# Sums of weights and of normed inputs on GpSimd, two more FFN pairs and one more head group in seven block products, in a two-layer trunk

## The chip, the core and the metric

The kernel runs on one core of a Trainium2 chip. The core has TensorE (PE, matmuls into PSUM), VectorE (DVE), ScalarE (ACT), GpSimd (POOL) and SyncE (SP, which only issues DMAs); each takes its own instructions in order and waits at semaphores for the others. The metric is the device time of one execution in microseconds, as the median of several runs.

## What is computed

A trunk of two layers over one sequence of 512 tokens with 1024 channels, in fp32. Layer 0 mixes tokens by attention, layer 1 by causal pooling; each is followed by a SwiGLU FFN with 2816 hidden channels, and everything stands behind RMSNorms:

```python
for i in range(DEPTH):                    # 2
    j = i // N_MIXERS
    if i % N_MIXERS == 0:
        x = x + dilated_attention_mixer(rmsnorm(x, attn_norm[j]), w_qkv[j], w_attn_out[j])
    else:
        x = x + pooling_mixer(rmsnorm(x, pool_norm[j]), w_pool_in[j], w_pool_group[j], pool_scale[j])
    x = x + swiglu_ffn(rmsnorm(x, ffn_norm[i]), w_ffn_gate_up[i], w_ffn_down[i])
return rmsnorm(x, final_norm)

def swiglu_ffn(h, w_gate_up, w_down):
    gu = h @ w_gate_up
    gate, up = gu[..., :D_FF], gu[..., D_FF:]
    return (jax.nn.silu(gate) * up) @ w_down
```

The attention has 8 heads of 128 channels in each of three groups (windows 128, 512, 2048 with dilations 1, 4, 16). In each head the outputs of the three groups are merged with weights from their softmax denominators.

## The kernel before

**Matmuls.** Every fp32 operand is split in two parts, hi and lo, of a reduced format: `split` copies hi on ACT (L77) and subtracts for lo on DVE (L78). Each product is three matmuls: hi x hi, hi x lo, lo x hi. A plain product (`Product.add`, L254, L255, L257) runs over 8 chunks of 128 channels with 512 tokens at a time.

**Seven block products.** Most products are made in pairs (gate and up of an FFN tile, q and k of a head and group) as a 2 x 2 block product with seven multiplications in place of eight (`seven`, matmuls at L371 to L373 with 256 tokens; `values12` with L483 to L485 for the values). It needs sums of the weight blocks and sums of the normed inputs. A weight pair (`Pair`) is loaded as tiles b, a and c by SP, a DMA issued on POOL (L137) accumulates a further block into b, and then four steps split them: `blocks` (a), `sums` (b), `more`, which first makes two sums in a (L150, L151) and splits it again (called the m split below), and `last` (c). The tiles lie in rings: five split weights (`w`), two halves, four raw tiles of 1024 columns (`raw`), two raw halves. A step runs when the ring has room, a load when the raw rings have. The sums of the inputs are made by `normed`: L434 scales two chunks of inputs into a raw tile h, and L438 to L440 make the sums in a raw tile t. The two functions `prepare`, one in the attention and one in `ffn`, call it for each of 4 pairs of chunks and split the results (h, t, tx in the attention; tb, tt, tn in the FFN).

**Plain ones.** The first pairs of each FFN (`NPLAIN`) and the first groups of head 1 (`NSOLO`) are plain, in the time in which the inputs for the seven block products are prepared. In the FFN one preparation is written after each plain pair.

**Attention.** The work of a head is laid into the products of the next one. `seven` and `values12` call functions at places counted by block products (`after`, filled by `between` and by the dictionary of head 7's values): `scores0` and `scores12` make scores and softmax parts, `merge` the weights of the groups (L614 on DVE puts the statistics in place, L618 on PE swaps partitions, L621 to L631 are small steps, L633 scales the scores of group 0 on DVE and L636 those of the others on ACT), `turn0` and `turn12` transpose (L645), `turn_values` transposes the values (L540), and `output` multiplies. L614 is issued behind the last instruction of the preceding evacuation (`mark`).

What stands where on an engine comes from a scheduler that takes the instructions as they become ready by their priority, so the written order is not the order on the engines.

Of the kernel before, what the change touches and what calls it, by code (L numbers as in the profile page):

```python
# [16 lines left out]
S = 512  # L17
# [15 lines left out]
NF = 4  # L33
H2 = S // 2
K2 = KC // 2
NPLAIN = 6
WARM = 6
NSOLO = 3
DOWN = (6, 5)
BUFS = {"w": 5, "half": 2, "raw": 4, "rawhalf": 2}  # L40
COLS = {"w": D, "half": D // 2, "raw": D, "rawhalf": D // 2}
# [7 lines left out]
def trunk(ctx: ExitStack, tc: tile.TileContext, xT, norms, w_first, w_qk, w_qkp, w_v0, w_v0p, w_v12, w_out, w_pair, w_down, w_pin, w_pgrp,  # L49
          consts, ident_in, invcnt_in, outT):  # L50
    nc = tc.nc
# [24 lines left out]
    def split(hi, lo, v):  # L76
        nc.scalar.activation(hi, v, AF.Copy)  # L77
        nc.vector.tensor_tensor(lo, v, hi.bitcast(F32), op=OP.subtract)  # L78
# [42 lines left out]
    class Pair:  # L121
# [25 lines left out]

        def more(self):
            a, b = self.a.t, self.b.t
            nc.vector.tensor_add(a[:, :S], a[:, :S], b[:, :S])  # L150
            nc.vector.tensor_add(a[:, S:], a[:, S:], a[:, :S])  # L151
            self.b.done()
            self.w["m"] = Held("w")
            split(*self.w["m"].t, a)
            self.a.done()
# [33 lines left out]
    for h in range(HEADS):  # L189
        if h == 0:  # L190
            plain(*[w_qk[u] for u in range(len(QK) - NF)])
        for g in range(3):
            if h == 1 and g < NSOLO:
                plain(*[w_qk[len(QK) - NF + 2 * g + c] for c in range(2)])
            elif h:
                pairs(w_qkp[3 * h - 3 - NSOLO + g])
        if h == 0:
# [7 lines left out]
    def ffn_plan(layer):  # L205
        for hf in range(2):
            for j in range(hf * HALF, (hf + 1) * HALF):
                if j < NPLAIN:
                    plain_gu(layer, j)
# [219 lines left out]
    def normed(layer, k, row):  # L429

        h, t = Held("raw"), Held("raw")
        for i in range(2):
            c = k + i * K2
            nc.vector.scalar_tensor_tensor(h.t[:, i * S:(i + 1) * S], X[c], nrm[:, layer, c:c + 1], row,  # L434
                                           op0=OP.mult, op1=OP.mult)
        hq = h.t.rearrange("p (a b c) -> p a b c", a=2, b=2)
        tq = t.t.rearrange("p (a b c) -> p a b c", a=2, b=2)
        nc.vector.tensor_sub(tq[:, :, 0], hq[:, :, 1], hq[:, 0])  # L438
        nc.vector.tensor_sub(t.t[:, H2:S], t.t[:, :H2], h.t[:, 3 * H2:])
        nc.vector.tensor_add(t.t[:, 3 * H2:], t.t[:, H2:S], h.t[:, S:3 * H2])  # L440
        return h, t

    def halves_of(hi, lo):
# [7 lines left out]
    with tc.tile_pool(name="opool", bufs=1) as opool:  # L451
        early = opool.tile([P, HEADS, S], F32R, tag="o", name="early")
        with tc.tile_pool(name="apool", bufs=1) as apool:
# [307 lines left out]
            def later(f, *a):  # L761
                return lambda: f(*a)

            def between(h, g):

                if g == 0:
                    return {1: [later(merge, h - 1)], 3: [later(turn_values, h - 1)] if h > 1 else []} if h % 2 else {
                        1: [later(output, h - 2)], 2: [later(merge, h - 1)]}
                if g == 1:
                    return {0: [later(turn0, h - 1)], 2: [later(turn12, h - 1)], 4: [later(scores0, h)]}  # L770
                return {2: [] if h % 2 else [later(output, h - 1)]}
# [19 lines left out]
            for h in range(1, HEADS):  # L791
                for g in range(3):
                    if h == 1 and g < NSOLO:
                        for c in range(2):
                            evac(h, 2 * g + c, product(0))
                        for fs in between(h, g).values():
                            for f in fs:
                                f()
                    else:
                        for c in range(2):  # L800
                            QKV[h, g, c] = apool.tile([P, S], F32, name=f"qk{g}{c}")
                        seven(T, QKV[h, g, 0], QKV[h, g, 1], scratch, between(h, g), g == 0)
                if h == 1:
                    whole = opool.tile([P, HEADS, S], F32, tag="o", name="o")
                    o.extend(whole[:, h, :] for h in range(HEADS))
                if h == HEADS - 1:
                    for key in [key for key in held if key[0] == "t"]:
                        give(key)
                    X[:] = [x_tile(k) for k in range(KC)]
                    for k in range(KC):  # L810
                        nc.gpsimd.dma_start(X[k], xT[:, k, :])
                if h % 2 == 0:
                    VT[:] = [apool.tile([P, S], F32, tag=tag, name="vt") for tag in ("row", "o0")]
                    seven(T, *VT, scratch, {0: [later(scores12, h)]}, True)
                elif h < HEADS - 1:
                    QKV[h // 2, 12, 2] = values12({0: [later(scores12, h)]})
                else:
                    QKV[h // 2, 12, 2] = values12({0: [later(scores12, h)], 1: [later(halve, 0), later(halve, 1)],
                                                   2: [later(merge, h), later(halve, 2), later(halve, 3)],
                                                   4: [later(halve, 4), later(halve, 5)]})  # L820
            for k in range(KC):
                give(("h", k))
# [29 lines left out]
    with tc.tile_pool(name="fpool", bufs=2) as fpool:  # L852
# [30 lines left out]
        def ffn(layer, nxt, lead, row):  # L883

            op = nxt - 1

            def gu():
                return lead.pop(0).p if lead else product(op)

            def hidden(j):  # L890
                return act[j]

            def plain_pair(last):
                pg = gu()
                gt = ftile("gt")
                nc.vector.tensor_mul(gt, pg, row)
                pu = gu()
                if last:
                    for k in range(KC):
                        give((op, k))  # L900
                up = ftile("up")
                nc.vector.tensor_mul(up, pu, row)
                activation(gt, up)

            T = {}

            def prepare(k):


                h, t = normed(op, k, row)  # L910
                hq, b22 = h.t.rearrange("p (a b c) -> p a b c", a=2, b=2), h.t[:, 3 * H2:]
                held["t", k, 0], b = slot("tb")
                split(b[:, 0].rearrange("p (a c) -> p a c", a=2), b[:, 1].rearrange("p (a c) -> p a c", a=2), hq[:, :, 0])
                T["11", k], T["21", k] = (tuple(b[:, e, i * H2:(i + 1) * H2] for e in range(2)) for i in range(2))
                for i, names in enumerate((("1", "2"), ("3", "4"))):
                    held["t", k, 1 + i], b = slot("tt")
                    split(b[:, 0], b[:, 1], t.t[:, i * S:(i + 1) * S])
                    for a, name in enumerate(names):
                        T[name, k] = tuple(b[:, e, a * H2:(a + 1) * H2] for e in range(2))
                if k % 2 == 0:  # L920
                    held["t", k, 3], T["n"] = slot("tn")
                n = tuple(T["n"][:, e, k % 2 * H2:(k % 2 + 1) * H2] for e in range(2))
                split(*n, b22)
                T["22", k] = n
                h.done()
                t.done()

            def strassen_pair():
                gt, up = ftile("gt"), ftile("up")
                seven(T, gt, up, ftile)  # L930
                activation(gt, up)

            for hf in range(2):
                act.clear()
                for j in range(hf * HALF, (hf + 1) * HALF):
                    if j < NPLAIN:
                        plain_pair(j == NPLAIN - 1)
                        if 0 < j <= K2:
                            prepare(j - 1)
                    else:  # L940
                        strassen_pair()
                early = [Product(HALF, hidden).add(range(HALF - 1)) for i in range(2)]
                if hf:
                    for key in [key for key in held if key[0] == "t"]:
                        give(key)
                for m in range(KC - 2 if nxt == 4 and hf else KC):
                    if early:
                        f = early.pop(0).add([HALF - 1])
                    else:
                        f = Product(HALF, hidden).add(range(HALF))  # L950
                    if hf and layer == 0:
                        unfold(m, f.p)
                    else:
                        nc.vector.tensor_add(X[m], X[m], f.p)
                    if hf:
                        note(nxt, m)
                if not (hf and nxt == 4):
                    for j in range(HALF):
                        give(("a", j))
            return hidden  # L960
# [118 lines left out]
        t = total(0, add(0, 0, end(0, 0, range(HALF))))  # L1079
# [4 lines left out]
        t = total(1, add(0, 1, f))  # L1084
# [80 lines left out]
```

## Time and profile before

| | |
|---|---|
| median of 3 runs | 1272.15 us (1271.86 to 1273.1) |
| profiled execution | 1271.68 us, span 1269.9 us |
| granted TensorE clock | 0.997 |
| PE busy | 1252.9 us, 99% |
| DVE busy | 922.3 us, 73% |
| ACT busy | 567.6 us, 45% |
| POOL busy | 127.2 us, 10% |
| HBM | 135 GB/s over the span |

The profile is one execution. A row of a timeline has the start in us, the duration in us, the engine, line and operation, output and inputs by name, and in brackets the idle time before it and what ended that. A row with x2 or more takes several equal instructions together. Rows of groups have duration in ns or busy time and the mean; the text ahead of them says which. PE's matmuls are pipelined, so that the distance from start to start is the pitch, and the duration in the row is longer.

### The profile page before, as it was taken

Reading aid. Unit: us, or ns where it says so; the run is one execution under the profiler, and the core shown is the slowest. Engines: PE = TensorE matmul, PEld = TensorE weight load, DVE = VectorE, ACT = ScalarE, POOL = GpSimd, SP = SyncE. Lnnn points to the kernel's source line nnn. Section 1 sums busy time; section 2 is a strip of 40 time slices with the busy share of each in tenths; the row PEclk is TensorE's granted clock in tenths of the full one; section 3 lists DMA queues with packets and bytes.
Section 4 is the critical chain, followed back from the end, with each engine's and each line's share of the span. In section 5 each row is a group of like instructions: output and inputs, shape, how many; then the busy total and the mean of one; then the engine's idle time right before and its main releaser. Section 6 shows DMA issues by size and latency. Waiting matters only on the chain.

```text
span 1269.9 us, 20876 instructions
## 1 busy us (share of the span) xinstructions
PE 1252.9 (99%) x8306; PEld 1154.4 (91%) x8306; DVE 922.3 (73%) x1383; ACT 567.6 (45%) x879; POOL 127.2 (10%) x121
## 2 busy tenths in 40 slices
PE   9999999999999999999999999999999999999997
PEld 7879999999999988889989999888788988999986
DVE  6977788878778846688636887558978853788643
ACT  6444554445445544444424554343444532455331
POOL 1011111102111000001001110000300000110000
PEclk9999999999999999999999999999999999999998
DMA  8335556655755444147446774333124645666322
GB/s 294 100 86 164 133 144 150 165 133 151 182 134 149 118 150 132 52 100 187 129 142 157 183 185 129 99 133 126 41 77 113 172 129 139 171 181 172 92 69 67
DMA packets 67330, 172.45 MB, mean 136 GB/s; under 512 B 6928, under 2 KB 9120, under 8 KB 67232
## 3 DMA queue, kind: packets, MB, share of 16 engines
q1 hardware_dynamic: 48816, 135.97, 33.4%
q0 software_dynamic: 17264, 34.09, 15.8%
q8 instruction: 65, 1.06, 0.3%
q10 hardware_dynamic: 1152, 1.05, 0.2%
q14 instruction: 33, 0.27, 0.1%
HBM read 168.99 MB, written 2.10 MB: 135 GB/s over the span
## 4 chain that ended last, share of the span: by engine, by line
PE 79%; issue 11%; DVE 7%; ACT 2%; POOL 1%; DMA 0%; DVEq 0%; POOLq 0%; ACTq 0%
PE ps L371 12%; PE ps L372 12%; PE ps L373 12%; PE ps L255 10%; PE ps L254 10%; PE ps L257 10%; PE ps L483 2%; PE ps L485 2%; PE ps L484 2%; DVE wlo L78 1%; PE ps L678 1%; PE ps L590 1%; ACT whi L77 1%; POOL rcol L323 1%; DVE n L302 1%
## 5 line engine op out<-in xcount | busy, mean ns | idle before, releaser
L77 ACT ACTIVATE whi<-raw 128x1024 fp32r<-128x1024 f32 (+2 forms) x297 | 295.9, 1001 | 427.7 <-PE ps L255 194.6
L78 DVE TENSOR_TENSOR wlo<-raw,whi 128x1024 fp32r<-128x1024 f32 (+2 forms) x297 | 340.5, 1150 | 153.5 <-ACT whi L77 152.1
L254 PE MATMUL ps<-a,whi 128*128 128x512 f32 (+1 forms) x374 | 141.0, 377 | 0.0
L255 PE MATMUL ps<-a,whi 128*128 128x512 f32 (+1 forms) x374 | 140.9, 377 | 0.0
L257 PE MATMUL ps<-a,wlo 128*128 128x512 f32 (+1 forms) x374 | 140.8, 377 | 0.0
L371 PE MATMUL ps<-tt,whi 128*128 128x256 f32 x384 | 108.7, 283 | 0.0
L372 PE MATMUL ps<-tt,whi 128*128 128x256 f32 x384 | 108.7, 283 | 0.0
L373 PE MATMUL ps<-tt,wlo 128*128 128x256 f32 x384 | 108.7, 283 | 0.0
L137 POOL DMA_DIRECT2D raw<-w_pair x32 | 38.7, 1209 | 445.3 <-DVE wlo L78 173.6
L257 PEld LDWEIGHTS ps<-a,wlo 128*128 128x128 f32 x374 | 70.4, 188 | 13.0
L254 PEld LDWEIGHTS ps<-a,whi 128*128 128x128 f32 x374 | 70.4, 188 | 12.8
L255 PEld LDWEIGHTS ps<-a,whi 128*128 128x128 f32 x374 | 70.4, 188 | 12.7
L372 PEld LDWEIGHTS ps<-tt,whi 128*128 128x128 f32 x384 | 73.7, 192 | 0.0
L371 PEld LDWEIGHTS ps<-tt,whi 128*128 128x128 f32 x384 | 73.7, 192 | 0.0
L373 PEld LDWEIGHTS ps<-tt,wlo 128*128 128x128 f32 x384 | 73.7, 192 | 0.0
L372 PE MATMUL ps<-tb,whi 128*128 128x256 f32 x256 | 72.5, 283 | 0.0
L371 PE MATMUL ps<-h,whi 128*128 128x256 f32 x252 | 72.5, 288 | 0.0
L373 PE MATMUL ps<-tb,wlo 128*128 128x256 f32 x256 | 72.5, 283 | 0.0
L371 PE MATMUL ps<-tb,whi 128*128 128x256 f32 x256 | 72.4, 283 | 0.0
L373 PE MATMUL ps<-h,wlo 128*128 128x256 f32 x252 | 71.3, 283 | 0.0
L372 PE MATMUL ps<-h,whi 128*128 128x256 f32 x252 | 71.3, 283 | 0.0
L254 PE MATMUL ps<-h,whi 128*128 128x512 f32 x160 | 62.7, 392 | 0.0
(280 smaller groups left out, 3423.4 us busy)
## 6 DMA issues: line engine op xcount, KB each, us to landing
raw<-w_pair SPq DMA_DIRECT2D x76, 512.0 KB, 4.3
raw<-w_qkp SPq DMA_DIRECT2D x36, 512.0 KB, 4.2
raw<-w_pair POOLq DMA_DIRECT2D x32, 512.0 KB, 7.2
raw<-w_down SPq DMA_DIRECT2D x32, 384.0 KB, 3.1
raw<-w_down SPq DMA_DIRECT2D x32, 320.0 KB, 2.8
raw<-w_v SPq DMA_DIRECT2D x18, 512.0 KB, 4.2
raw<-w_qkp POOLq DMA_DIRECT2D x18, 512.0 KB, 7.0
rawhalf<-w_pair SPq DMA_DIRECT2D x32, 256.0 KB, 3.4
```

The source lines that it names most:

```text
L77: nc.scalar.activation(hi, v, AF.Copy)
L78: nc.vector.tensor_tensor(lo, v, hi.bitcast(F32), op=OP.subtract)
L137: nc.gpsimd.dma_start(self.b.t.rearrange("p (a c) -> p a c", a=2), self.src[:, None, 3 * S:].to_broadcast([P, 2, S]), accum_op=OP.add)
L254: nc.tensor.matmul(self.p[:, cols], w[0][:, s], mh[:, cols], start=self.done == 0, stop=False)
L255: nc.tensor.matmul(self.p[:, cols], w[0][:, s], ml[:, cols], start=False, stop=False)
L257: nc.tensor.matmul(self.p[:, cols], w[1][:, s], mh[:, cols], start=False, stop=self.done == self.n)
L371: nc.tensor.matmul(dst, w.t[0][:, c], th, start=k == 0, stop=False)
L372: nc.tensor.matmul(dst, w.t[0][:, c], tl, start=False, stop=False)
L373: nc.tensor.matmul(dst, w.t[1][:, c], th, start=False, stop=k == K2 - 1)
L483: nc.tensor.matmul(o, mh, wh, start=k == 0, stop=False)
L484: nc.tensor.matmul(o, mh, wl, start=False, stop=False)
L485: nc.tensor.matmul(o, ml, wh, start=False, stop=k == K2 - 1)
```

## The change

Three things are moved to GpSimd or shifted. The sums L150, L151 and L438 to L440 run on GpSimd in place of VectorE. One more pair of each FFN and one more group of head 1 are made by seven block products. And in the attention the merge after an odd head's start and the turn of the values are placed one block product later, in head 7 the merge is too, and in the FFN each preparation is written one plain pair earlier.

```diff
-NPLAIN = 6
+NPLAIN = 5
-NSOLO = 3
+NSOLO = 2
...
         def more(self):
             a, b = self.a.t, self.b.t
-            nc.vector.tensor_add(a[:, :S], a[:, :S], b[:, :S])
-            nc.vector.tensor_add(a[:, S:], a[:, S:], a[:, :S])
+            nc.gpsimd.tensor_add(a[:, :S], a[:, :S], b[:, :S])
+            nc.gpsimd.tensor_add(a[:, S:], a[:, S:], a[:, :S])
...
-        nc.vector.tensor_sub(tq[:, :, 0], hq[:, :, 1], hq[:, 0])
-        nc.vector.tensor_sub(t.t[:, H2:S], t.t[:, :H2], h.t[:, 3 * H2:])
-        nc.vector.tensor_add(t.t[:, 3 * H2:], t.t[:, H2:S], h.t[:, S:3 * H2])
+        nc.gpsimd.tensor_sub(tq[:, :, 0], hq[:, :, 1], hq[:, 0])
+        nc.gpsimd.tensor_sub(t.t[:, H2:S], t.t[:, :H2], h.t[:, 3 * H2:])
+        nc.gpsimd.tensor_add(t.t[:, 3 * H2:], t.t[:, H2:S], h.t[:, S:3 * H2])
...
-                    return {1: [later(merge, h - 1)], 3: [later(turn_values, h - 1)] if h > 1 else []} if h % 2 else {
+                    return {2: [later(merge, h - 1)], 4: [later(turn_values, h - 1)] if h > 1 else []} if h % 2 else {
...
-                                                   2: [later(merge, h), later(halve, 2), later(halve, 3)],
+                                                   2: [later(halve, 2), later(halve, 3)], 3: [later(merge, h)],
...
                     if j < NPLAIN:
                         plain_pair(j == NPLAIN - 1)
-                        if 0 < j <= K2:
-                            prepare(j - 1)
+                        if j < K2:
+                            prepare(j)
```

The order of the instructions on the engines shows what it moves. First TensorE in head 3, in the first group's products, before:

```order
918 L373 MATMUL ps<-h,wlo 128x256
919 L371 MATMUL ps<-h,whi 128x256
920 L372 MATMUL ps<-h,whi 128x256
921 L373 MATMUL ps<-h,wlo 128x256
922 L371 MATMUL ps<-t,whi 128x256
923 L372 MATMUL ps<-t,whi 128x256
924 L373 MATMUL ps<-t,wlo 128x256
925 L618 MATMUL ps<-far,const 128x32 x2
926 L371 MATMUL ps<-t,whi 128x256
```

And the same place now (t and tx are the sums of the inputs, far the statistics from L614):

```order
959 L373 MATMUL ps<-h,wlo 128x256
960 L371 MATMUL ps<-t,whi 128x256
961 L372 MATMUL ps<-t,whi 128x256
962 L373 MATMUL ps<-t,wlo 128x256
...
969 L371 MATMUL ps<-tx,whi 128x256
970 L372 MATMUL ps<-tx,whi 128x256
971 L373 MATMUL ps<-tx,wlo 128x256
972 L618 MATMUL ps<-far,const 128x32 x2
973 L371 MATMUL ps<-t,whi 128x256
```

The swap stood behind three matmuls with t, and stands behind twelve. On VectorE the instruction that it waits for, L614, had a sum of weights ahead of it:

```order
188 L425 TENSOR_TENSOR vt<-ps,sums 128x4x32x4
189 L426 TENSOR_TENSOR vt<-sums,ps 128x2x32x4
190 L150 TENSOR_TENSOR raw<-raw 128x512
191 L614 TENSOR_TENSOR far<-st,place 128x64
192 L151 TENSOR_TENSOR raw<-raw 128x512
```

Now a lo split stands there:

```order
161 L425 TENSOR_TENSOR vt<-ps,sums 128x4x32x4
162 L426 TENSOR_TENSOR vt<-sums,ps 128x2x32x4
163 L78 TENSOR_TENSOR halflo<-rawhalf,halfhi 128x512
164 L614 TENSOR_TENSOR far<-st,place 128x64
165 L78 TENSOR_TENSOR wlo<-raw,whi 128x1024
```

The sums left VectorE there, and L614 keeps one instruction of that size ahead of it. On GpSimd, from the first RMSNorm (L323) to head 2, there stood before:

```order
10 L323 TENSOR_TENSOR rcol<-var,nhalf 128x4
11 L554 TENSOR_SCALAR b_812<-const 128x256
12 L555 TENSOR_SCALAR b_812<-const 128x128
13 L137 DMA raw<-w_v 128x2x512
14 L558 TENSOR_SCALAR b_815<-const 128x128 x2
15 L137 DMA raw<-w_v 128x2x512
```

There now, of the same stretch, the part from the accumulating DMA of the first pair (the first pair is that of head 1's third group, so its weights are w_qkp):

```order
20 L137 DMA raw<-w_v 128x2x512
21 L150 TENSOR_TENSOR raw<-raw 128x512
22 L151 TENSOR_TENSOR raw<-raw 128x512
23 L438 TENSOR_TENSOR raw<-raw 128x2x256
24 L558 TENSOR_SCALAR b_824<-const 128x128
25 L439 TENSOR_TENSOR raw<-raw 128x256
26 L558 TENSOR_SCALAR b_824<-const 128x128
27 L440 TENSOR_TENSOR raw<-raw 128x256
28 L438 TENSOR_TENSOR raw<-raw 128x2x256
29 L439 TENSOR_TENSOR raw<-raw 128x256
30 L440 TENSOR_TENSOR raw<-raw 128x256
```

The sums of the first pair and of the third and fourth preparations follow each other in one queue, with the slopes of the next head's scores (L558) between them.

## The prediction

> **What bounds the kernel now.** I read the page first, then the waits of TensorE, then a stretch of seven-block products by engine, then TensorE's rows around its waits. The busy time of each engine:
>
> ```profile
> PE 1252.9 (99%) x8306; PEld 1154.4 (91%) x8306; DVE 922.3 (73%) x1383; ACT 567.6 (45%) x879; POOL 127.2 (10%) x121
> ```
>
> TensorE (PE) is the bound: 1252.9 of 1269.9 us. A change can win in two ways only: less matmul time, or fewer of the few waits PE has. The waits of PE, in whole us, times and longest:
>
> ```profile
> PE ps L618 <- DVE far L614: 3.2, 4, 0.9
> PE ps L645 <- ACT s L636: 1.6, 1, 1.6
> PE ps L540 <- DVE nm L575: 0.2, 1, 0.2
> ```
>
> They add up to little, and the largest is the swap of the merge (L618), four times. In the long stretches of seven-block products PE waits for nothing, with VectorE (DVE) at 87%:
>
> ```profile
> core 0: us, PE busy (x) PEld busy (x) DVE busy (x) ACT busy (x) POOL busy (x), PEclk, DMA share, GB/s
> 696.82:747.22 50.40, 50.40 (x422) 50.40 (x421) 43.64 (x62) 26.24 (x35) 6.02 (x5) 1.00 0.72 183
> ```
>
> That stretch is five pairs of the second half of the first FFN, so DVE works 43.64/5 = 8.73 us of each pair's 10.08. Relief of DVE there is worth nothing; only the places where PE waits for DVE count.
>
> **The change part by part.**
>
> *Three more seven-block products in place of plain ones.* The rows give the pitch of each kind:
>
> ```profile
> 520.08 0.39 PE L254 MATMUL ps<-h,whi 128*128 128x512 f32 x1
> 520.76 0.39 PE L254 MATMUL ps<-h,whi 128*128 128x512 f32 x1
> 600.03 0.28 PE L371 MATMUL ps<-tb,whi 128*128 128x256 f32 x1
> 600.39 0.28 PE L371 MATMUL ps<-tb,whi 128*128 128x256 f32 x1
> ```
>
> Three matmuls of 512 columns take 0.68 us, three of 256 columns 0.36. A plain pair has 2 x 8 x 3 = 48 matmuls, 48 x 0.2267 = 10.88 us; a seven-block pair has 7 x 4 x 3 = 84, 84 x 0.12 = 10.08. One pair in each FFN layer and one group of head 1: 3 x 0.80 = **-2.4 us**. Here nothing hides the gain, for PE is the bound.
>
> *The merges one block product later.* The first fence shows PE around the swap of head 3 and what DVE does before it, the second PE at head 7:
>
> ```profile
> 172.87 0.28 PE L373 MATMUL ps<-t,wlo 128*128 128x256 f32 x1
> 173.91 0.60 PE L618 MATMUL ps<-far,const 128*128 128x32 f32 x4 [0.76 <-DVE far L614]
> 172.47 0.65 DVE L426 TENSOR_TENSOR vt<-sums,ps 128x256 f32<-128x256 f32 x1
> 172.95 0.69 DVE L150 TENSOR_TENSOR raw<-raw 128x512 f32<-128x512 f32 x1
> 173.56 0.21 DVE L614 TENSOR_TENSOR far<-st,place 128x64 f32<-128x64 f32 x1
> ```
>
> ```profile
> 435.66 0.28 PE L485 MATMUL ps<-whi,tx 128*128 128x256 f32 x1
> 436.82 0.60 PE L618 MATMUL ps<-far,const 128*128 128x32 f32 x4 [0.88 <-DVE far L614]
> ```
>
> A start gap of 1.04 less the pitch of 0.12 is 0.92 us of standing, at each of the odd heads (three of the four waits); at head 7 it is 1.16 - 0.12 = 1.04. In the order of the changed kernel nine more matmuls stand ahead of the swap at the odd heads, 9 x 0.12 = 1.08 us, and twelve at head 7, 1.44 us. Both are more than the wait, so up to 3 x 0.92 + 1.04 = 3.8 us go. The margin at the odd heads is only 0.16: L150 has left DVE, but a lo split of the same shape now stands in its place ahead of L614, and if GpSimd (POOL) is adding just then, DVE is late by about 0.8 to 1.0 (priced below). POOL will be adding for about a third of the time, so I take off 3 x 0.33 x 0.84 = 0.8: **-3.0 us**, with ends of -1.0 (head 7 alone) and -3.8.
>
> *The sums on POOL instead of DVE.* What they cost on DVE, and the nearest rows of POOL (the page's duration columns; in the first five min/median/max in ns):
>
> ```profile
> L150 DVE TENSOR_TENSOR raw<-raw x61: 678/682/795, 77.9 to 1175.5; 128x512 f32<-128x512 f32 x61
> L438 DVE TENSOR_TENSOR raw<-raw x12: 677/686/693, 40.9 to 975.7; 128x512 f32<-128x512 f32 x12
> L439 DVE TENSOR_TENSOR raw<-raw x12: 409/424/429, 42.1 to 976.9; 128x256 f32<-128x256 f32 x12
> L292 POOL TENSOR_TENSOR acc<-sq 128x512 f32<-128x512 f32 x1 | 1.3, 1330 | 27.3 <-ACT sq L287 27.3
> L1069 POOL TENSOR_TENSOR x<-xg,row 128x256 f32<-128x256 f32 x2 | 1.4, 736 | 1.3 <-ACT row L1065 1.3
> L137 POOL DMA_DIRECT2D raw<-w_pair x32 | 38.7, 1209 | 445.3 <-DVE wlo L78 173.6 <-DMA raw<-w_pair 122.4 <-DVE raw L150 43.3
> ```
>
> L151 is like L150, and L440 like L439. DVE is rid of 2 x 0.682 = 1.37 us per pair and of 0.69 + 2 x 0.42 = 1.53 per prepared pair of chunks. POOL pays 1.33 for 128x512 and 0.74 for 128x256 where it works alone: 2.66 per pair, 2.81 per preparation. The rows where both work at once say more:
>
> ```profile
> 889.41 1.50 DVE L302 SCALAR_TENSOR_TENSOR n<-x,nrm,n 128x512 fp32r<-128x512 f32 x2
> 903.37 2.44 DVE L302 SCALAR_TENSOR_TENSOR n<-x,nrm,n 128x512 fp32r<-128x512 f32 x2
> 905.75 1.75 DVE L1002 TENSOR_TENSOR s<-u 128x512 f32<-128x512 f32 x1
> 896.25 0.66 DVE L1002 TENSOR_TENSOR s<-s 128x512 f32<-128x512 f32 x1
> 903.48 3.47 POOL L292 TENSOR_TENSOR acc<-acc,sq 128x512 f32<-128x512 f32 x2 [11.43 <-ACT sq L287]
> ```
>
> Under two POOL adds that took 3.47 together, DVE's two-input work lost 2.44 - 1.50 = 0.94 and 1.75 - 0.66 = 1.09: about 1.0 us for each POOL add, and POOL's own add grew from 1.33 to 1.74. So per pair in the steady stretch DVE goes from 8.73 to 8.73 - 1.37 + 2 x 1.0 = 9.36 of 10.08, and POOL from 1.21 (its accumulating DMA) to 1.21 + 3.47 = 4.7. Both still fit: **0 us** there. In POOL's queue each accumulating DMA now stands behind an earlier pair's sums, at most 3.5 us later; the rest of the period covers it.
>
> The Trainium skill, GPSIMD Engine Reference, section 4.1, puts two-input elementwise work on VectorE and calls GPSIMD about twice as slow; the rows agree (1.33 against 0.68) and add the stretch to 1.74. The rule speaks against the change, and by it each sum costs 0.65 us more where it lies on the path; the trace says that it mostly does not.
>
> *Where a sum does lie on the path.* Two lead-ins, where preparations, splits and the first pair come close together.
>
> First, heads 0 and 1:
>
> ```profile
> 39.16 1.21 DVE L78 TENSOR_TENSOR wlo<-raw,whi 128x1024 fp32r<-128x1024 f32 x1
> 55.46 1.08 DVE L461 TENSOR_TENSOR vt<-ps,row 128x512 f32<-128x512 f32 x1
> 56.60 0.66 PE L540 MATMUL ps<-ident,vt 128*128 128x128 f32 x4 [0.21 <-DVE nm L575]
> 79.13 0.39 PE L257 MATMUL ps<-early,wlo 128*128 128x512 f32 x1
> 81.13 1.12 PE L645 MATMUL ps<-ident,s 128*128 128x128 f32 x6 [1.61 <-ACT s L636]
> ```
>
> The split that ends at 40.37 frees the first buffer for L438. From there POOL is done with L439 at 42.5 and L440 at 43.2, and ScalarE and DVE, whose next instructions in order are the splits of those sums, stand until then. Following the new order with the durations above (second preparation's sums from 47.6 to 50.4, four splits, L565, L571, the first vt), the second vt ends near 58.0 instead of 56.54, and the transposes L540 behind it move by 1.4. Further on, L438 of the third preparation now waits for the lo split of the first pair's sums (near 71.9), then two 128x128 instructions of L558 stand between its parts on POOL, so that its last part ends near 76.2; L434 of the fourth waits for that; its sums run from 78.8 to 81.6, its last split ends near 82.9, and behind it on DVE stands L633, the scaling that L645 needs. PE's L645 then starts near 83.4 instead of 81.13. The 1.4 is inside this: **+2.3 us**. That is with POOL at its lone rate, since DVE mostly stands while POOL works. At the stretched rate, each preparation takes (3.47 - 2.66)/2 = 0.4 longer for the long part and about as much for the two short ones, twice in a row: +3.9. The other end is +1, if the order of waits lets half of it go under PE.
>
> Second, the start of the seven-block pairs in each FFN. The preparations are written one plain pair earlier and the plain pairs are one fewer, so one plain pair still lies between the last preparation and the first block product:
>
> ```profile
> 541.16 0.39 PE L254 MATMUL ps<-h,whi 128*128 128x512 f32 x1
> 557.48 0.39 PE L254 MATMUL ps<-h,whi 128*128 128x512 f32 x1
> 568.36 0.28 PE L371 MATMUL ps<-tb,whi 128*128 128x256 f32 x1
> ```
>
> With one plain pair fewer the first block product starts at 557.48 instead of 568.36, and needs the fourth chunk's tb after nine matmuls, at 558.56 and its lo part 0.12 later. The pair's s split gets its buffer when the product ends at 541.16, and is behind the sums of the second preparation on ScalarE: 543.2. Then DVE in its new order, from 544.3: s lo split 1.2, a 0.6, two L434 1.4, tb, tn, up 1.6, m lo split 1.2 (550.9); POOL's three sums 2.8 (553.7); the fourth L434's two parts with three splits between 3.2 (556.9); a weight's lo split 1.2 and tb 0.6: 558.7. That is just in time, with no slack. The tt of the next sums (561.0 at the latest) are not needed before 561.4. With a stretch of 1.0 it is late by that: I take 0.2 per layer, **+0.4 us**, with ends 0 and 2 x 2.0.
>
> Sum: -2.4 - 3.0 + 2.3 + 0.4 = **-2.7 us**. The profiled execution of before took 1271.68 (span 1269.9 and 1.78 around it), 0.47 below the median 1272.15; so 1269.0 against the profile, and **1269.4** as a median.
>
> **The rivals.**
>
> *Lead-ins at the stretched rate.* DVE's splits have two inputs from memory like L302, so POOL's sums and DVE's splits stretch each other there too: -2.4 - 3.0 + 3.9 + 2 x 2.0 = +2.5, 1274.7. For it: no slack at 558.7. Against: DVE stands idle for much of POOL's time in those chains.
>
> *Slower: DVE becomes the bound in the seven-block pairs of the FFN.* The point is a loss of (10.08 - 7.36)/2 = 1.36 us of DVE per POOL add. If DVE loses the whole 1.74 of each, it needs 7.36 + 3.47 = 10.83 per pair, 0.75 too much; over the 34 seven-block pairs of the two FFNs at most 25 us, and about a third of that, 8, once the weights split ahead are used up and the down products let DVE catch up. With the sum: -2.7 + 8 = +5.3, 1277.5. For it: the rows lose up to 1.09 with one DVE instruction, and two in a row may each lose. Against: 0.94 over two.
>
> The Trainium skill, SBUF — State Buffer, section "SBUF: two separate sides", says that of a VectorE instruction with two SBUF inputs and a GpSimd one the second is blocked until the first has ended. By that rule the loss would be up to the lone 1.33 per add, 10.02 per pair, and PE would stay the bound by 0.06; the 0.94 and 1.09 above lie below it.
>
> *The lead-ins are covered.* POOL works at its lone rate, the swaps lose nothing, and other work of PE hides all but 0.5 of the two lead-ins: -2.4 - 3.8 + 0.5 = -5.7, 1266.4.
>
> *The swaps still wait*, since L614 moves along: -2.4 - 1.0 + 2.7 = -0.7, 1271.5.
>
> **How the numbers follow.** Forecast 0.36, covered lead-ins 0.17, stretched lead-ins 0.22, DVE as the bound 0.15, waiting swaps 0.10. A run tells about 0.2% (2.5 us) from no change: faster is below 1269.6, slower above 1274.7. The forecast lies at that edge, so about 0.27 of its 0.36 counts as faster and the rest as the same; with 0.17 of the covered case and a little of the others faster is 0.46. Of the stretched case half is slower, and with DVE as the bound and its worse ends that makes 0.31; the same has 0.23. The range goes from the covered case with no cost in the lead-ins (1272.15 - 6.2 = 1265.9) to the middle of the case with DVE as the bound: 1265.5 to 1278.
>
> **What would show it.** PE's wait at L618 gone or under 1 us in all; L645 near 83.4; the first block product of the FFN within 0.5 us of the last plain product; POOL rows for L150 of 1.3 to 1.8 us, and DVE's splits beside them longer than 1.22. It is wrong if PE shows waits at lo splits (L373 for wlo) in the middle of the pairs, or if L645 or the first tb waits by several us.

## The result: 1.5% slower

The changed kernel takes 1291.55 us (median of 4 runs, 1289.83 to 1292.62) against 1272.01 before: ratio 1.0151, 95% interval 1.0133 to 1.0168. The forecast was 1269.4 with a range of 1265.5 to 1278. The profiled execution took 1292.62 us with a span of 1290.7 and a granted clock of 0.988 (before 0.997). The first part of its page:

```profile
PE 1259.5 (98%) x8414; PEld 1164.8 (90%) x8414; DVE 911.2 (71%) x1237; ACT 570.0 (44%) x888; POOL 361.2 (28%) x288
```

VectorE is relieved by 11 us only, GpSimd works 234 us more, and PE is busy 6.6 us longer although it has 2.4 us less matmul work. So its matmuls ran slower, by 9.0 us in all. (The kernel with the same pairs and all sums on VectorE, below, keeps VectorE busy for 928.3 us. Against it the relief is 17 us, where sums of some 106 us left VectorE: 64 weight pairs at 1.37 and 12 preparations at 1.53.) The waits of PE that are new or longer:

```profile
PE ps L645 <- DVE s L633: 6.7, 1, 6.7
PE ps L371 <- ACT tb L77: 6.1, 2, 3.0
PE ps L540 <- DVE vt L461: 2.5, 2, 1.5
PE ps L590 <- DVE qk L425: 2.4, 3, 0.8
PE ps L372 <- DVE tb L78: 1.2, 2, 0.7
```

L618 is gone from the list, as forecast. The two lead-ins stand at its head in its place: the transposes of head 0 (L645) and the first tb of both FFNs. What is not in this list is the granted clock, in windows of PE around these waits (start and end, length, busy time of PE, clock):

```profile
core 0: us, PE busy (x), PEclk, DMA share, GB/s
90.00:95.00 5.00, 4.54 (x24) 0.66 0.67 161
95.00:100.00 5.00, 5.00 (x44) 1.00 0.28 50
567.00:571.00 4.00, 0.95 (x9) 1.00 0.01 2
571.00:576.00 5.00, 4.34 (x19) 0.52 0.00 0
576.00:580.00 4.00, 4.00 (x28) 0.74 0.41 135
```

After the wait of 3.0 us at the FFN start PE runs at half clock for 6.8 us: in windows of 1 us the clock is 0.50 from 572 to 578 and 0.98 in the next one. By the windows above (1 - 0.52) x 4.34 + (1 - 0.74) x 4 = 3.1 us are lost besides the waits themselves; the second FFN has the same wait and again 6.8 us at half clock. The Trainium skill, TensorE: Matmul & The Clock Gate, part 1, says that an idle window of about 3.4 us halves the clock and a busy one restores it; here a wait of 3.0 us was enough, and the half clock lasted 6.8 us.

To place the loss, each run below is cut at the same TensorE instructions, counted from its first matmul with the layer's input: to the first L590 of head 1 (heads 0 and 1), to the L318 of the first FFN's norm (heads 2 to 7 and the output), and each FFN from its norm to the next one. The lengths of these stages less those of the kernel before, in us, from one profiled execution each:

| kernel | heads 0, 1 | heads 2 to 7 | FFN 0 | FFN 1 |
|---|---|---|---|---|
| changed kernel | +10.4 | -0.4 | +6.1 | +5.7 |
| all sums on VectorE | +5.1 | -1.1 | -0.5 | -0.6 |
| inputs' sums on VectorE | +3.4 | -0.3 | +0.6 | +0.4 |
| weights' sums on VectorE | +7.5 | -1.1 | +2.5 | +3.3 |
| merges only | +0.3 | -1.1 | +0.1 | +0.3 |
| all on VectorE, three plain groups | +0.4 | -1.1 | -0.5 | -0.6 |
| changed, three plain groups | +8.3 | -0.4 | +5.7 | +5.4 |
| only the sums on GpSimd | +7.9 | +2.9 | +6.3 | +4.3 |
| copies of all sums on GpSimd | +7.1 | +0.9 | +8.5 | +8.6 |
| GpSimd work that nobody waits for | +3.5 | -1.1 | +6.7 | +6.0 |
| longer wait at L645 | +7.5 | 0.0 | +0.2 | -0.1 |

### The profile page after: what moved, and what is told of

Read it like the earlier page. It is cut to its first block, busy times and chain, and to the rows that moved or that the text cites. A ratio compares the mean times of both kernels' runs of the same rounds, so it can differ in the third digit from the quotient of the medians.

```text
span 1290.7 us, 21292 instructions
## 1 busy us (share of the span) xinstructions
PE 1259.5 (98%) x8414; PEld 1164.8 (90%) x8414; DVE 911.2 (71%) x1237; ACT 570.0 (44%) x888; POOL 361.2 (28%) x288
## 4 chain that ended last, share of the span: by engine, by line
PE 74%; issue 11%; DVE 8%; POOL 4%; ACT 1%; DMA 1%; SPq 0%; DVEq 0%; POOLq 0%; ACTq 0%
PE ps L372 14%; PE ps L371 14%; PE ps L373 14%; PE ps L255 7%; PE ps L254 7%; PE ps L257 7%; PE ps L483 2%; PE ps L484 2%; PE ps L485 2%; DVE wlo L78 2%; DVE raw L434 1%; PE ps L678 1%; POOL raw L438 1%; PE ps L590 1%; POOL raw L439 1%
## 5 line engine op out<-in xcount | busy, mean ns | idle before, releaser
L78 DVE TENSOR_TENSOR wlo<-raw,whi 128x1024 fp32r<-128x1024 f32 (+2 forms) x300 | 380.4, 1270 | 177.1 <-ACT whi L77 175.9
L371 PE MATMUL ps<-tt,whi 128*128 128x256 f32 x408 | 116.6, 286 | 0.0
L372 PE MATMUL ps<-tt,whi 128*128 128x256 f32 x408 | 116.5, 286 | 0.0
L373 PE MATMUL ps<-tt,wlo 128*128 128x256 f32 x408 | 116.4, 285 | 0.0
L150 POOL TENSOR_TENSOR raw<-raw 128x512 f32<-128x512 f32 x64 | 89.6, 1399 | 95.6 <-DVE wlo L78 87.8
L151 POOL TENSOR_TENSOR raw<-raw 128x512 f32<-128x512 f32 x64 | 99.0, 1547 | 5.0
L371 PE MATMUL ps<-tb,whi 128*128 128x256 f32 x272 | 78.4, 288 | 6.1 <-ACT tb L77 6.1
L372 PE MATMUL ps<-tb,whi 128*128 128x256 f32 x272 | 78.6, 289 | 1.2 <-DVE tb L78 1.2
L371 PEld LDWEIGHTS ps<-tt,whi 128*128 128x128 f32 x408 | 79.6, 195 | 0.0
L372 PEld LDWEIGHTS ps<-tt,whi 128*128 128x128 f32 x408 | 79.6, 195 | 0.0
L373 PEld LDWEIGHTS ps<-tt,wlo 128*128 128x128 f32 x408 | 79.5, 195 | 0.0
L373 PE MATMUL ps<-tb,wlo 128*128 128x256 f32 x272 | 78.3, 288 | 0.0
L371 PE MATMUL ps<-h,whi 128*128 128x256 f32 x264 | 76.2, 289 | 0.0
L373 PE MATMUL ps<-h,wlo 128*128 128x256 f32 x264 | 74.6, 283 | 0.0
```

Source lines behind the costliest of these rows:

```text
L150: nc.gpsimd.tensor_add(a[:, :S], a[:, :S], b[:, :S])
L151: nc.gpsimd.tensor_add(a[:, S:], a[:, S:], a[:, :S])
L371: nc.tensor.matmul(dst, w.t[0][:, c], th, start=k == 0, stop=False)
L372: nc.tensor.matmul(dst, w.t[0][:, c], tl, start=False, stop=False)
L373: nc.tensor.matmul(dst, w.t[1][:, c], th, start=False, stop=k == K2 - 1)
```

## The experiments

**Which part of the change makes it.** The theory after the result (A): the sums on GpSimd make the lead-ins late, by stretching VectorE's splits and by the waits for the sums. Its rival (B): the lead-ins became too short, whoever makes the sums. The first three kernels start from the changed one and take the sums back to VectorE: all in the first, those of the inputs in the second, those of the weights in the third. One line of each kind:

```diff
-            nc.gpsimd.tensor_add(a[:, :S], a[:, :S], b[:, :S])
+            nc.vector.tensor_add(a[:, :S], a[:, :S], b[:, :S])
...
-        nc.gpsimd.tensor_sub(tq[:, :, 0], hq[:, :, 1], hq[:, 0])
+        nc.vector.tensor_sub(tq[:, :, 0], hq[:, :, 1], hq[:, 0])
```

All on VectorE: 

> The changed kernel with all sums back on VectorE: two more FFN pairs and one more group of head 1 in seven block products, merges later, preparations one plain pair earlier. Theory A (the sums on GpSimd, through their stretch of VectorE's splits and through the waits for them, make the lead-ins late): the waits at L645 and at the first tb go back to about 2 and under 1 us, no slow clock, and the time is 1272.0 - 2.4 - 1 to 3 = 1267 to 1269. Theory B (the lead-ins are simply too short for the seven block products that now start earlier, whoever makes the sums): the waits of 3 us at both FFN starts and of 6 us at L645 stay, 1285 to 1292.

Measured 1274.91, ratio 1.0021 (1.0012 to 1.0031), between the two forecasts. Both FFNs came out as A says, 0.5 to 0.6 us shorter than before, with no wait at tb. Heads 0 and 1 came out as B says, 5.1 us longer, with a wait of 5.3 at L645 and no GpSimd sum anywhere. So the two lead-ins differ: the FFNs lose nothing once the sums are back, and heads 0 and 1 are late without them too.

Inputs' sums back: 

> The changed kernel with only the sums of the normed inputs (L438 to L440) back on VectorE, the sums of the weights still on GpSimd. Theory A, with the inputs' sums as the main part (4 x 2.8 us of GpSimd in each lead-in, and VectorE and ScalarE wait for them): most of the loss goes, 1269 to 1275. If the weights' sums are what makes the lead-ins late, it stays above 1283. Theory B: 1285 to 1292.

Measured 1276.58 (1.0032, 1.0020 to 1.0043), just above A's range. The weights' sums alone on GpSimd cost about 1 us in each FFN and 0.8 in the heads 2 to 7, and save 1.6 in heads 0 and 1.

Weights' sums back: 

> The changed kernel with only the sums of the weights (L150, L151) back on VectorE, the sums of the inputs still on GpSimd. Theory A with the inputs' sums as the main part: most of the loss stays, 1283 to 1290, with the wait at L645 above 4 us and at the first tb above 2 us. If the weights' sums are the main part: 1268 to 1275. Theory B: 1285 to 1292.

Measured 1284.50 (1.0094, 1.0079 to 1.0109). The inputs' sums alone cost 3.0 and 4.0 us in the FFNs and 2.5 in heads 0 and 1, against the kernel with all on VectorE. The wait at the first tb is 1.7 us in each FFN, under the 2 expected. Both kinds together cost 6.6 and 6.3: more than the two parts' sum, 4.1 and 5.0. What is more is the clock: with both it is halved for 6.8 us in each FFN (3.1 lost), with the inputs' sums alone only in the second, for 3.4 us (1.7 lost), with the weights' sums alone in neither. Without that it is 3.5 and 3.2 against 4.1 and 3.3.

**The later merges alone.**

```diff
-                    return {1: [later(merge, h - 1)], 3: [later(turn_values, h - 1)] if h > 1 else []} if h % 2 else {
+                    return {2: [later(merge, h - 1)], 4: [later(turn_values, h - 1)] if h > 1 else []} if h % 2 else {
...
-                                                   2: [later(merge, h), later(halve, 2), later(halve, 3)],
+                                                   2: [later(halve, 2), later(halve, 3)], 3: [later(merge, h)],
```

> The kernel before with only the later places of the merges and of the turn of the values. If the swap's wait goes and nothing takes its place: -3.0 to -3.8, 1268.2 to 1269.0. In the changed kernel three waits of 0.8 us at L590 for the product's last evacuation (L425) stand where the three waits at L618 had gone: if the later place makes them, -1.0 to -1.5, 1270.5 to 1271; if the sums on GpSimd make them, they are absent here.

Measured 1271.46 (0.9993, 0.9984 to 1.0003): only head 7's 1.1 us came. At the odd heads the wait stays, for L614 moved along. VectorE's rows at head 3 in this kernel, and PE's:

```profile
172.94 0.69 DVE L150 TENSOR_TENSOR raw<-raw 128x512 f32<-128x512 f32 x1
173.56 0.68 DVE L78 TENSOR_TENSOR halflo<-rawhalf,halfhi 128x512 fp32r<-128x512 f32 x1
174.15 0.68 DVE L151 TENSOR_TENSOR raw<-raw 128x512 f32<-128x512 f32 x1
174.75 0.21 DVE L614 TENSOR_TENSOR far<-st,place 128x64 f32<-128x64 f32 x1
175.11 0.60 PE L618 MATMUL ps<-far,const 128*128 128x32 f32 x4 [0.77 <-DVE far L614]
```

Three instructions of that size stand ahead of it now, where it was one. With the weights' sums off VectorE and the merges later, as in the changed kernel, it is one again, and there L618 does not wait. But there the same sums make the wait at L590, as VectorE, GpSimd and PE show at head 2 of the changed kernel:

```profile
167.30 2.19 DVE L78 TENSOR_TENSOR wlo<-raw,whi 128x1024 fp32r<-128x1024 f32 x1 [0.26 <-ACT whi L77]
169.41 0.68 DVE L425 TENSOR_TENSOR qk<-ps,sums 128x512 f32<-128x512 f32 x1
167.11 1.30 POOL L151 TENSOR_TENSOR raw<-raw 128x512 f32<-128x512 f32 x1
170.14 1.05 PE L590 MATMUL ps<-qk,qk 128*128 128x128 f32 x7 [0.80 <-DVE qk L425]
```

The lo split took 2.19 in place of 1.21, since L151 of GpSimd ran beside it; L425 behind it was late, and PE with it. In the kernels with the weights' sums on VectorE this wait is absent.

**Head 1's group.**

```diff
-NSOLO = 2
+NSOLO = 3
```

First with all sums on VectorE: 

> The changed kernel with all sums on VectorE and head 1 as before (two plain groups and not one fewer: NSOLO 3), so that one more FFN pair per layer and the later merges are left. In the run with all sums on VectorE the stages were: heads 0 and 1 +5.4 us since the first matmuls, heads 2 to 7 -1.1, each FFN -0.5 to -0.6. If the one more group of head 1 alone makes the +5.4 (its weight pair takes two of the four raw tiles that the preparations need), this kernel is at 1272.1 - 1.1 - 0.5 - 0.6 = 1269.9, faster than before. If the lead-in of the heads is late for another reason (merges, order), it stays at 1274 to 1275.

Measured 1270.88, ratio 0.9987 (0.9978 to 0.9995): better than both kernels, by little. The 5.1 us of heads 0 and 1 (5.4 in the expectation) are down to 0.4. What the one more group does is seen in VectorE's third preparation, first with two plain groups, then with three:

```profile
66.04 1.23 DVE L78 TENSOR_TENSOR wlo<-raw,whi 128x1024 fp32r<-128x1024 f32 x1 [0.72 <-ACT whi L77]
67.30 1.42 DVE L434 SCALAR_TENSOR_TENSOR raw<-x,nrm,row 128x512 f32<-128x512 f32 x2
```

```profile
58.39 1.43 DVE L434 SCALAR_TENSOR_TENSOR raw<-x,nrm,row 128x512 f32<-128x512 f32 x2
```

Its L434 starts 8.9 us later, directly behind a lo split of the first weight pair. The program gives the pair two of the four raw tiles, so the preparation has to wait until one is free; that this is the reason was read from the order and not tried by itself.

Then with the sums on GpSimd: 

> The changed kernel, sums on GpSimd, with head 1 as before (NSOLO 3). If count and sums add up in heads 0 and 1 (+5.4 for the group and some +4 for the sums), 1291.5 - 5 = 1286 to 1287. If the sums alone make the wait at L645 (theory of the first prediction's rival), 1290 to 1291, and it stays near 6 us.

Measured 1290.16 (1.0137, 1.0123 to 1.0151): the time that was expected of the sums alone, though the wait at L645 is 4.2 us and not near 6. Two causes do not add up here: with the sums on GpSimd heads 0 and 1 are 8.3 us late even with three plain groups, and the group adds 2.1 more, where it added 4.7 with all on VectorE.

**The sums alone.** The kernel before with the two edits of `more` and `normed` and nothing else:

> The kernel before with nothing but the sums on GpSimd: six plain pairs, three plain groups, merges and preparations as before. If the shorter lead-in of the FFN is needed for the loss, each FFN is within 1 us of before and only the heads' lead-in loses (+4 to +7): 1276 to 1280. If the sums on GpSimd lose 5 us and more at the FFN whatever the number of plain pairs: 1286 to 1292.

Measured 1293.05 (1.0162, 1.0145 to 1.0179). The sums on GpSimd are the loss by themselves; six plain pairs, with the preparations written one pair later as before, do not save the FFN (+6.3 and +4.3; PE's wait at the first tb is 2.7 us in the first and 2.6 in the second, and only behind the first is the clock halved, for 6.8 us). Both old waits are there together: L618 four times, 2.9 us, and the new L590 three times, 2.4.

**Stretch or waiting?** Two kernels give GpSimd work that nobody waits for, on top of all sums on VectorE with three plain groups (1270.88). The first repeats every sum into an unused tile:

```diff
+            extra = tmp.tile([P, S], F32, tag="sq", name="extra")
+            for o in (0, S):
+                nc.gpsimd.tensor_tensor(extra, b[:, o:o + S], b[:, o:o + S], op=OP.subtract)
```

and likewise behind the inputs' sums. 

> The kernel with all sums on VectorE, one more FFN pair per layer, later merges and three plain groups in head 1, to which GpSimd work is added that nobody waits for: for every sum an operation of the same size that reads the same raw tile and writes an unused tile. It has the stretch without the chain of waits. If the stretch of VectorE's splits is what makes the FFN starts late, each FFN is 2 to 4 us longer than without the additional work, 1274 to 1278; if it is the chain (VectorE and ScalarE waiting for GpSimd's sums), it stays within 1 us of the kernel without them, about 1270 to 1271.

Measured 1299.50 (1.0207, 1.0193 to 1.0221), worse than the changed kernel and above both forecasts. It isn't clean: VectorE waited twice for a raw tile that the added work was still reading:

```profile
DVE raw L441 <- POOL extra L154: 5.0, 2, 2.5
```

The second reads the layer's row in its place, and of the raw tile only four columns ahead:

```diff
+        extra = tmp.tile([P, S], F32, tag="sq", name="extra")
+        nc.gpsimd.tensor_tensor(extra[:, :4], h.t[:, S:S + 4], h.t[:, S:S + 4], op=OP.subtract)
+        for c in (S, H2, H2):
+            nc.gpsimd.tensor_tensor(extra[:, :c], row[:, :c], row[:, :c], op=OP.subtract)
```

> The kernel with all sums on VectorE, one more FFN pair per layer, later merges and three plain groups in head 1 (1270.9), with GpSimd work beside each preparation that nobody waits for and that holds no raw tile but for a short first read: one read of 4 columns of h, then 512, 256 and 256 columns subtracted from the layer's row into an unused tile. VectorE's order is unchanged. If stretch alone makes the lead-ins late: VectorE's splits beside it take up to twice their time, and each FFN and the heads' lead-in get 1 to 3 us longer, 1273 to 1279. If it is the waits for GpSimd's results: within 1 us, 1270 to 1272.

Measured 1287.00 (1.0111, 1.0096 to 1.0126), above both forecasts. In its trace neither VectorE nor ScalarE waits for GpSimd once, and VectorE's order is that of the kernel without the work. Yet the FFNs are 7.3 and 6.6 us longer than there. The first and the last L434 of the first FFN's preparations in this kernel, with the split of tb and what PE does at that place; then the same two L434 without the work:

```profile
530.14 1.41 DVE L434 SCALAR_TENSOR_TENSOR raw<-x,nrm,row 128x512 f32<-128x512 f32 x2
561.34 1.41 DVE L434 SCALAR_TENSOR_TENSOR raw<-x,nrm,row 128x512 f32<-128x512 f32 x2
564.62 1.10 DVE L78 TENSOR_TENSOR tb<-raw,tb 128x512 fp32r<-128x512 f32 x1
563.47 0.38 PE L371 MATMUL ps<-tb,whi 128*128 128x256 f32 x1 [2.80 <-ACT tb L77]
565.77 0.58 PE L372 MATMUL ps<-tb,whi 128*128 128x256 f32 x1 [1.92 <-DVE tb L78]
```

```profile
527.41 1.41 DVE L434 SCALAR_TENSOR_TENSOR raw<-x,nrm,row 128x512 f32<-128x512 f32 x2
554.84 1.41 DVE L434 SCALAR_TENSOR_TENSOR raw<-x,nrm,row 128x512 f32<-128x512 f32 x2
557.37 0.69 DVE L78 TENSOR_TENSOR tb<-raw,tb 128x512 fp32r<-128x512 f32 x1
```

From the first L434 to the last it takes 31.2 us in place of 27.4, and to the end of the split of tb 35.6 in place of 30.7: 4.9 us late. In both kernels VectorE is idle for about 1 us of that time; the difference is in its busy time, 34.6 against 29.7, so the stretch alone makes the preparation late. PE waits 4.7 us in all, and the rest of the 7.3 is the slower clock. So stretch is enough; waiting for GpSimd's results is not needed.

In the changed kernel there are waits for them too:

```profile
DVE raw L434 <- POOL raw L440: 12.9, 5, 3.0
```

In the first FFN VectorE stands 3.0 and 2.8 us for this and loses 3.8 by stretch (its rows are shown with the prediction's steps), while its own sums, 6.6 us in that time, are gone; the first tb is split 34.6 us after the first L434, against 30.7 with all on VectorE. So both have a part there. How much of the loss would be left with one of them was not tried.

**The clock after a wait.** Two tries on the kernel before, to make PE wait longer at one place and nothing else.

The first has three passes ahead of L633:

```diff
+                for i in range(STALL if h == 0 else 0):
+                    nc.vector.tensor_scalar(s0, s0, 1.0, None, op0=OP.mult)
```

> The kernel before with three more passes of VectorE over head 0's scores (multiplied by 1.0, 128x896 each) ahead of L633, so that TensorE waits at L645 about 3 us longer (4.6 in place of 1.6), and nothing else is changed. If a wait costs only itself: +3 us, 1275. If TensorE is granted a slower clock for some us after a wait of more than about 2 us, as the rows behind the long waits of the changed kernel say: +3 and 1.5 to 3 more, 1276.5 to 1278, with a granted clock under 0.8 in the 5 us behind the wait.

Measured 1271.54 (0.9990, 0.9980 to 0.9999): the three passes do not depend on the merge and stood far ahead of it in the order, so that the wait came out at 0.9 us and not longer. It says nothing on the clock. In the second try the four passes stand behind L633.

> The kernel before with four passes of VectorE over head 0's scores (multiplied by 1.0, 128x896, 0.6 us each in the run before) behind L633, which TensorE's L645 then waits for; two lo splits of 1.2 us come between them in the order. The wait grows from 1.6 to about 6 us. If a wait costs only itself, TensorE is +4 to +5 us late and behind L645 no later than that: 1276 to 1277. If a slower granted clock follows a long wait, 1.5 to 3 us more, 1278 to 1280, with a granted clock near 0.5 in the 5 us behind it.

Measured 1279.56 (1.0056, 1.0040 to 1.0071). PE's longest wait (L648 is the L645 of the other kernels), and the clock in the windows behind it:

```profile
PE ps L648 <- DVE s L636: 7.2, 1, 7.2
```

```profile
core 0: us, PE busy (x), PEclk, DMA share, GB/s
88.00:93.00 5.00, 5.00 (x22) 0.68 0.29 70
93.00:98.00 5.00, 5.00 (x23) 1.00 0.48 75
```

The transposes start 5.3 us late, at 86.3, and the first L590 of head 1 is 7.5 us late: 2.2 us were lost behind the wait. The clock is 0.50 from 86.3 to 91.2, so that it alone takes 2.5 (the 0.68 is of a window that starts later and ends behind it). The wait cost itself and some 2 us more.

The price is not fixed, however. In all these runs the clock is halved within or just behind every wait of PE of 3.0 us and more in a lead-in, for 3.4, 6.8 or 10.2 us, and 1.5 to 3.2 us are lost by it. With shorter waits it goes either way: halved behind 2.7 us at the first FFN and not behind 2.6 at the second (only the sums on GpSimd), not behind 1.7 at the first and halved behind 1.7 at the second (weights' sums on VectorE).

## Why the prediction was wrong, step by step

- *Three more pairs, -2.4.* The two in the FFN came to -0.5 and -0.6 each with all sums on VectorE. The one in head 1 had the wrong sign: +4.7 (5.1 against 0.4) in place of -0.8, by its raw tiles as far as the order tells. The walk through the order had seen L438 wait for the pair's last split, and counted it as GpSimd's cost.
- *The swaps, -3.0.* Right in itself: all four waits at L618 are gone. But three waits of 0.8 at L590, at the scores of heads 2, 4 and 6, took their place, by a stretched lo split. Heads 2 to 7 gained 0.4.
- *Nothing in the steady stretch.* Right: no wait at a weight's lo split in the middle of the pairs, and the rival by which VectorE becomes the bound there did not come true. In five pairs' 50.4 us (from 711 on in the changed kernel) VectorE is busy 42.9 us, 8.58 a pair where the walk had 9.36: each of GpSimd's sums costs it 0.6 us there, not 1.0. That is still nearly all that it was rid of, for before it was 8.73.
- *The lead-ins, +2.3 and +0.4.* This is the step that failed: heads 0 and 1 came to +10.4 and the FFNs to +6.1 and +5.7, where the sum had +1.5 and twice -0.6 (the -0.8 of a pair included). I took GpSimd's lone rate, "since DVE mostly stands while POOL works". It stands at L434, and the walk had that in, but behind it VectorE's splits run beside GpSimd's sums. Both engines at the second preparation of the first FFN:

```profile
548.47 2.00 DVE L78 TENSOR_TENSOR wlo<-raw,whi 128x1024 fp32r<-128x1024 f32 x1
550.40 1.22 DVE L78 TENSOR_TENSOR tb<-raw,tb 128x512 fp32r<-128x512 f32 x1
551.78 2.71 DVE L78 TENSOR_TENSOR tt<-raw,tt 128x512 fp32r<-128x512 f32 x2 [0.15 <-ACT tt L77]
554.40 1.51 DVE L78 TENSOR_TENSOR tn<-raw,tn 128x256 fp32r<-128x256 f32 x1
549.47 1.60 POOL L439 TENSOR_TENSOR raw<-raw 128x256 f32<-128x256 f32 x1
552.18 1.75 POOL L150 TENSOR_TENSOR raw<-raw 128x512 f32<-128x512 f32 x1
```

  Alone these VectorE rows take 1.22, 0.69, 1.28 and 0.42, as in the kernel before: 3.8 us are lost here, in one preparation, under sums of both kinds. The walk put the first tb at 558.7; counted from the same L434 the changed kernel had it some 4 us later. Nearly all of it comes from this place, as the s split behind it shows, with the split of tb:

```profile
552.79 1.04 ACT L77 ACTIVATE whi<-raw 128x1024 fp32r<-128x1024 f32 x1
557.04 1.21 DVE L78 TENSOR_TENSOR wlo<-raw,whi 128x1024 fp32r<-128x1024 f32 x1
571.34 0.69 DVE L78 TENSOR_TENSOR tb<-raw,tb 128x512 fp32r<-128x512 f32 x1
```

  The first L434 is 9.2 us later in this profile than in that of before. With that, ScalarE is within 0.4 us of the walk (543.2), and VectorE is 3.5 us behind it (544.3); from there to the end of the split of tb it took 15.0 us and the walk had 14.4. The walk had no slack, so PE waits 3.0 and 0.7 us, and with 3.1 for the clock and -0.8 for the pair that makes 6.0 of the +6.1. In heads 0 and 1 the sums of the third preparation began at 75.0 where the walk had 71.9, behind two waits at L540 and 3.4 us of half clock. Then the fourth was stretched, and L633 behind it:

```profile
83.71 2.26 POOL L439 TENSOR_TENSOR raw<-raw 128x256 f32<-128x256 f32 x1
87.48 1.56 DVE L78 TENSOR_TENSOR tx<-raw,tx 128x512 fp32r<-128x512 f32 x1
88.96 2.07 DVE L633 TENSOR_SCALAR s<-s,co 128x256 f32<-128x256 f32 x4
90.45 0.88 PE L645 MATMUL ps<-ident,s 128*128 128x128 f32 x3 [6.66 <-DVE s L633]
```

  L645 at 90.4 and not 83.4; L439 took 2.26 where 0.74 was assumed. Here the stretch is not the only cause: with all sums on VectorE the wait at L645 is 5.3 us too, from the one more group, and with three plain groups and the sums on GpSimd it is 4.2. The rival of stretched lead-ins had the mechanism, but 2.0 us per FFN where about 4 came, and no clock. The prediction's own sign of being wrong, that L645 or the first tb waits by several us, is what came.
- *What was in no sum.* The granted clock. PE's busy time rose by 9.0 us over what its work explains, nearly half of the loss. In the profile before, PE's longest wait was 1.6 us at a clock of 1.00, so the profile did not show the price of a longer one. The rule of the Trainium skill (TensorE: Matmul & The Clock Gate, part 1) told of a clock that halves after an idle window, and I did not bring it to bear on the late ends.

The rule of the Trainium skill that spoke against the change (GPSIMD Engine Reference, section 4.1) had the sign right. Its factor of two for GpSimd's own duration was in the walk already, though; what the walk lacked was the loss of VectorE beside it.

## What to carry to other kernels

Moving elementwise work to GpSimd need not relieve VectorE where VectorE's own instructions read two operands from SBUF. Here some 106 us of sums left it and it was relieved by 17, for its splits were stretched, and the stretch landed where the slack is least, in the lead-in of a stage, however idle VectorE is on average. Before such a move, look for the places where preparation, splits and the bound engine meet with no slack, and price them at the stretched rate and in both directions. And price a wait of TensorE of 3 us and more with the slower clock behind it, which here cost 1.5 to 3.2 us more; with a wait of 1.7 to 2.7 us it may come or not.

## What the runs showed of the hardware that was not expected

A GpSimd instruction on four columns (L442), which takes 0.2 us in five of its twelve places, took 3.33 us while VectorE ran splits and sums without a pause, and up to 5.4 us in the heads (the kernel with work that nobody waits for):

```profile
531.64 0.19 POOL L442 TENSOR_TENSOR extra<-raw 128x4 f32<-128x4 f32 x1 [7.72 <-DVE raw L434]
540.43 3.33 POOL L442 TENSOR_TENSOR extra<-raw 128x4 f32<-128x4 f32 x1 [5.71 <-DVE raw L434]
```

So GpSimd is held back too, and not in proportion to its work. The Trainium skill, SBUF — State Buffer, section "SBUF: two separate sides", has the second of two such instructions blocked until the first has ended; an instruction that is held through several of VectorE's is more than that one sentence says. A short VectorE step was also hit: L625 on 128x8 took 1.24 us beside L438 of GpSimd in the changed kernel, where it takes 0.15 to 0.17 in the kernel before.
